# Row norms through GpSimd's power and device memory, and gate rows spread by DMA, in a two-layer fp32 trunk

## The chip, the cores and the metric

One core of a Trainium2 chip runs the whole trunk in one launch. TensorE (PE) multiplies, VectorE (DVE) and ScalarE (ACT) work on tiles, GpSimd (POOL) does masks and fills, and SyncE (SP) issues most transfers. The metric is the device time in microseconds.

## The reference

Input is x of 512 positions by 1024 channels and a memory of 256 positions. Each of two layers adds to x a mixer, an attention over the memory and a gated feed-forward net with a convolution of 3 taps. The mixer of layer 0 is forgetting attention (8 heads) beside differential attention (4 heads); that of layer 1 is an mLSTM of 4 heads. All is float32. What the change touches is how often this is computed, and the rows that go with the heads:

```python
def rms_norm(x, gain):
    x32 = x.astype(jnp.float32)
    y = x32 * lax.rsqrt(jnp.mean(x32 * x32, axis=-1, keepdims=True) + RMS_EPS)
    return (y * gain.astype(jnp.float32)).astype(x.dtype)
...
        logits = logits + F_b[..., :, None] - F[..., None, :]      # forgetting attention
...
        h = num / jnp.maximum(jnp.abs(den), jnp.exp(-m_t))[..., None]   # mLSTM
```

There is a norm ahead of each mixer, memory attention and feed-forward net, one of the memory in each layer, one of each differential head (128 channels), one of each mLSTM head (256 channels), and one at the end. In forgetting attention F is the running sum of a head's log gates; in the mLSTM, m is a running maximum over the positions.

## The kernel before

Activations lie transposed, channels on the 128 partitions and the 512 positions along the free axis, as eight tiles x. A float32 product is made from three matmuls in a reduced format: each operand is split into hi (a cast on ACT) and lo (a subtraction on DVE, L279), and `mm3` (L287 to 291) multiplies hi by hi, hi by lo and lo by hi. So each weight tile comes by a transfer that SP issues (`raw`), becomes `wh` on ACT (L282, L1183, L1352) and `wl` on DVE, each in three buffers, and then goes to PE.

The stages follow one another: mix0 (to about 263 us), xattn0 (to 404), ffn0 (to 740), mix1 (to 963), xattn1 (to 1104), ffn1 (to 1440) and the final norm with the writes. In mix0 four differential heads and four pairs of forgetting heads run beside the preparation of the memory and of both layers' memory keys. In an ffn, 22 blocks of gate and up projections (L1247 to L1420) and their down projections run; most blocks use a Strassen-like scheme of seven products (`c`, `ah`, `al`, `v`, `sa`, `sb` are its tiles).

Two planners write the order. `Plan` (mixers, xattn) takes items with a PE duration, dependences, priorities, buffers and a chain of costs on the other engines; `Sched` (ffn) takes a task for each engine. Both choose by these planned costs what is emitted next; each engine then runs its own queue strictly in order, and an instruction that waits holds all behind it.

A norm of x begins with the squares, summed over the eight tiles into `sq` on DVE (L486). The sum over the partitions and the root go so: four matmuls 128x2 with a matrix of ones put the sums in columns (L417, in the ffn L1218); DVE scales them (L426) and finds the inverse root with three Newton steps (L427 to 432, eleven small instructions more) as a tile of 128x4, position by position. DVE splits that into rh and rl and multiplies each into a diagonal of 128x512 (L446); two matmuls with ones spread it over all partitions (L452); ACT copies it out as `rb` (L456). The projections run on x without the norm, which is multiplied in when their sums leave PSUM (L1057 in xattn, L1317 in the ffn, L1519 in the mLSTM), and there DVE waits for `rb`. The heads' norms go the same way and are read straight from PSUM.

A gate row is spread over the partitions by PE too: `split_rows` (L594 to 604) writes hi and lo into a tile, DVE writes a selector (L611), PE multiplies (L612) and ACT copies the row out (L889 for forgetting heads, L1556 for the mLSTM's `mxb`, L1561 with an exponential for `emt`). On POOL run the causal masks of these rows (L900, L1573). The memory's norm is computed in both layers, from the same squares.

## Time and profile before

| | |
|---|---|
| median of three runs | 1455.0 us (1451.02, 1455.0, 1483.01) |
| profiled execution | 1451.45 us, span 1449.6 us |
| granted TensorE clock | 0.998 |
| PE, PEld, DVE, ACT, POOL busy | 98%, 87%, 82%, 55%, 4% |
| ffn0 and ffn1 | 404 to 740 us and 1104 to 1440 us |

The span is from the first to the last instruction. In rows of a timeline the columns are start, duration, engine, line, operation, output and inputs, shape, and in brackets the idle time of the engine before it with what ended that. In rows of groups, after the bar, stand busy time, mean ns of one, and idle time with its releasers. Matmuls overlap, so a record's duration is longer than the step from one matmul to the next. The trace shows one fp32 matmul as two records.

### The profile page before, as it was taken

The numbers are of one execution on the slowest core, as the hardware profiler recorded it, in microseconds if no ns is written. First come the engines' busy times: TensorE is split into PE (matmuls) and PEld (weight loads), VectorE is DVE, ScalarE is ACT, GpSimd is POOL, SyncE is SP. The second block draws the span as 40 slices with busy tenths as digits, with TensorE's granted clock in tenths as the row PEclk, the third lists the DMA queues.
The fourth block names the chain that finished last, engine by engine and source line by source line (L and its number), as shares of the span: only waits on it lengthen the run. The fifth ranks groups of instructions, "written<-read, shape, count | busy, mean of one in ns | idle before, by whom it ended". The sixth has DMA issues, their size and how long they took to land.

```text
span 1449.6 us, 22210 instructions
## 1 busy us (share of the span) xinstructions
PE 1423.5 (98%) x8330; PEld 1266.7 (87%) x8330; DVE 1189.9 (82%) x2255; ACT 798.5 (55%) x1345; POOL 58.4 (4%) x100
## 2 busy tenths in 40 slices
PE   9999999999999999999999999999999999999998
PEld 7888868899888999989888788889988899998997
DVE  7778886766689999989778868677667999999985
ACT  7767574444466555545456734444445665554544
POOL 0000120000001000000000100000000000000000
PEclk9999999999999999999999999999999999999999
DMA  5222305323247565642332232324323765654322
GB/s 201 88 73 73 102 30 160 117 88 131 83 142 198 152 170 163 164 127 68 90 102 87 74 102 74 116 88 129 119 81 130 187 168 162 172 153 134 92 70 80
DMA packets 60795, 171.74 MB, mean 118 GB/s; under 512 B 6672, under 2 KB 6672, under 8 KB 60688
## 3 DMA queue, kind: packets, MB, share of 16 engines
q1 hardware_dynamic: 55072, 152.43, 32.5%
q0 software_dynamic: 4608, 16.78, 6.9%
q8 instruction: 65, 1.06, 0.3%
q10 hardware_dynamic: 1008, 1.12, 0.2%
q14 instruction: 42, 0.34, 0.1%
HBM read 168.21 MB, written 2.10 MB: 117 GB/s over the span
## 4 chain that ended last, share of the span: by engine, by line
PE 72%; DVE 19%; issue 4%; ACT 3%; DMA 2%; POOL 0%; SPq 0%; DVEq 0%; ACTq 0%; POOLq 0%
PE acc L289 14%; PE acc L291 14%; PE acc L290 14%; DVE wl L279 4%; PE w L289 4%; PE w L291 4%; PE w L290 4%; DVE c L1281 3%; PE acc L351 2%; PE acc L352 2%; PE acc L353 2%; PE s L289 2%; PE s L291 2%; PE s L290 2%; PE w L1620 1%
## 5 line engine op out<-in xcount | busy, mean ns | idle before, releaser
L289 PE MATMUL acc<-xh,wh 128*128 128x512 f32 (+1 forms) x832 | 293.6, 353 | 4.2 <-ACT v L1390 4.2
L291 PE MATMUL acc<-xh,wl 128*128 128x512 f32 (+1 forms) x832 | 289.0, 347 | 0.0
L290 PE MATMUL acc<-xl,wh 128*128 128x512 f32 (+1 forms) x832 | 289.0, 347 | 0.0
L279 DVE TENSOR_TENSOR wl<-raw,wh 128x1024 fp32r<-128x1024 f32 (+2 forms) x201 | 240.3, 1196 | 38.0 <-ACT wh L282 35.8
L282 ACT CAST wh<-raw 128x1024 fp32r<-128x1024 f32 (+2 forms) x137 | 140.3, 1026 | 155.8 <-PE acc L290 96.8
L289 PEld LDWEIGHTS acc<-xh,wh 128*128 128x128 f32 x832 | 158.2, 190 | 19.5 <-ACT v L1390 4.8
L291 PEld LDWEIGHTS acc<-xh,wl 128*128 128x128 f32 x832 | 158.1, 190 | 15.3
L290 PEld LDWEIGHTS acc<-xl,wh 128*128 128x128 f32 x832 | 158.3, 190 | 14.4
L1281 DVE SCALAR_TENSOR_TENSOR c<-hs,vec,c 128x512 f32<-128x512 f32 x176 | 128.8, 745 | 6.6 <-ACT c L1274 6.2
L289 PE MATMUL w<-ah,wh 128*128 128x512 f32 x304 | 115.4, 380 | 0.0
L290 PE MATMUL w<-al,wh 128*128 128x512 f32 x304 | 115.3, 379 | 0.0
L291 PE MATMUL w<-ah,wl 128*128 128x512 f32 x304 | 115.3, 379 | 0.0
L1274 ACT ACTIVATE c<-hs,vec 128x512 f32<-128x512 f32 x88 | 67.9, 808 | 64.2 <-DVE hs L1419 57.1
L291 PEld LDWEIGHTS w<-ah,wl 128*128 128x128 f32 x304 | 57.5, 189 | 8.1
L290 PEld LDWEIGHTS w<-al,wh 128*128 128x128 f32 x304 | 57.6, 190 | 6.7
L289 PEld LDWEIGHTS w<-ah,wh 128*128 128x128 f32 x304 | 57.7, 190 | 6.7
L1295 ACT CAST ah<-c 128x512 fp32r<-128x512 f32 x44 | 27.3, 620 | 65.7 <-DVE c L1291 65.6
L289 PE MATMUL acc<-mem,wh 128*128 128x256 f32 (+1 forms) x192 | 60.3, 314 | 0.0
L291 PE MATMUL acc<-mem,wl 128*128 128x256 f32 (+1 forms) x192 | 59.7, 311 | 0.0
L290 PE MATMUL acc<-mem,wh 128*128 128x256 f32 (+1 forms) x192 | 59.6, 311 | 0.0
L512 DVE TENSOR_TENSOR x<-w,x 128x512 f32<-128x512 f32 x72 | 49.1, 682 | 7.9 <-PE w L291 7.8
L512 DVE TENSOR_TENSOR x<-acc,x 128x512 f32<-128x512 f32 x32 | 22.0, 690 | 40.4 <-PE acc L291 40.4
(373 smaller groups left out, 3766.0 us busy)
## 6 DMA issues: line engine op xcount, KB each, us to landing
raw<-in_up_dram SPq DMA_DIRECT2D x56, 512.0 KB, 3.3
dr<-in_down_dram SPq DMA_DIRECT2D x64, 256.0 KB, 3.4
sa<-in_up_dram SPq DMA_DIRECT2D x32, 512.0 KB, 4.2
sa<-in_up_dram POOLq DMA_DIRECT2D x32, 512.0 KB, 5.5
raw<-in_xk_dram SPq DMA_DIRECT2D x16, 512.0 KB, 3.3
raw<-in_wo_dram SPq DMA_DIRECT2D x16, 512.0 KB, 3.3
raw<-in_xq_dram SPq DMA_DIRECT2D x16, 512.0 KB, 3.3
raw<-in_xv_dram SPq DMA_DIRECT2D x16, 512.0 KB, 3.3
```

The lines of the kernel that those rows point to most:

```text
L279: self.nc.vector.tensor_tensor(out=lo, in0=v, in1=hi.bitcast(F32), op=ALU.subtract)
L282: self.nc.scalar.copy(hi, v)
L289: mm(out, wh, xh, start=first, stop=False, skip_group_check=parts)
L290: mm(out, wh, xl, start=False, stop=False, skip_group_check=parts)
L291: mm(out, wl, xh, start=False, stop=last, skip_group_check=parts)
L351: mm(ps, xh[k][:, ts], wh, start=(k == 0), stop=False)
L352: mm(ps, xh[k][:, ts], wl, start=False, stop=False)
L353: mm(ps, xl[k][:, ts], wh, start=False, stop=(k == 7))
L512: self.nc.vector.tensor_tensor(out=x, in0=restored(ps[:]), in1=x, op=ALU.add)
L1274: nc.scalar.activation(st["c_"][:, j, :], hs()[:, j, 2:514], AF.Identity, scale=self.col("cw", (layer * 3 + 2) * 44 + blk), bias=self.col( ...
L1281: nc.vector.scalar_tensor_tensor(out=c, in0=hs()[:, j, n : n + 512], scalar=w, in1=c, op0=ALU.mult, op1=ALU.add)
L1295: nc.scalar.copy(acts[p][0][:], u())
```

## The change

Eleven of the norms are computed "by rows": those of the four differential heads, of mLSTM heads 0 to 2, and of both layers' xattn and ffn. The summed squares are split into hi and lo (ACT, DVE), two matmuls 128x512 with ones sum them (every partition gets the sums as a row), ACT writes one row of 512 with scale and epsilon, an ACT transfer turns it to 128x4, POOL raises it to the power -0.5, a POOL transfer writes it to device memory, and an SP transfer spreads it over 128 partitions. The remaining norms (first, memory, mix1's, mLSTM head 3, final) stay spread by PE, with POOL's power in place of the Newton steps.

The eight forgetting rows and the mLSTM's two sets of four rows go to device memory by POOL and come back spread by SP, one transfer for a head. The exponential of `emt` is taken once, on four rows. The memory norm is computed in layer 0 only; its roots are kept in device memory and spread again in layer 1. In the ffn the norm is scheduled with a priority ahead of the blocks instead of after the first one. In the plans a chain may hold a pure delay ("-"): 2.7 us for a small transfer and 5.0 for a spread.

```diff
+ROW_DMA, SPREAD_DMA = 2.7, 5.0
...
+    def p_row_norm(self, pl, state, scale, eps, to, fin, deps=(), prio=None, fdeps=(), chain=()):
+
+        nc, sp = self.nc, self.sp
+        st = {}
+
+        def parts():
+            st["p"] = self.row_parts(state["sq"])
+
+        def sums():
+            st["row"] = self.row_sums(st["p"], scale, eps)
+
+        def turned():
+            st["z"] = self.row_turned(st["row"])
+
+        def spread():
+            st["rb"] = self.row_spread(st["d"], to)
+
+        a = pl.add(parts, 0, deps, prio, chain=(("A", 0.52), ("D", 0.6)))
+        a = pl.add(sums, 0.43, [a], prio, take=("s",), free=("s",), chain=(("A", 0.5),))
+        a = pl.add(turned, 0, [a], prio, chain=(("-", ROW_DMA),))
+        a = pl.add(lambda: st.update(d=self.row_root(st["z"])), 0, [a], prio, chain=(("G", 1.05), ("-", ROW_DMA)))
+        a = pl.add(spread, 0, [a], prio, chain=(("-", SPREAD_DMA),))
+        return pl.add(lambda: fin(st["rb"]), 0, [a, *fdeps], prio, chain=chain)
+
+    def row_parts(self, sq):
+        hi, lo = (self.til(self.sp, "sqt", dtype=F32R) for _ in range(2))
+        self.split(hi[:], lo[:], sq[:])
+        return hi, lo
+
+    def row_sums(self, parts, scale, eps):
+        ps = self.bank("b")
+        for i, part in enumerate(parts):
+            self.nc.tensor.matmul(banked(ps[:]), self.onesr[:], alternate(part[:]), start=i == 0, stop=i == 1)
+        row = self.til(self.sp, "sqt")
+        self.nc.scalar.activation(folded(row[0:1, :]), restored(ps[0:1, :]), AF.Copy, scale=float(scale), bias=float(eps))
+        return row
+
+    def row_turned(self, row):
+        z = self.til(self.sp, "z", (P, 4))
+        self.nc.scalar.dma_start(z[:], row[0:1, :].rearrange("o (p j) -> o p j", j=4))
+        return z
+
+    def row_root(self, z):
+        y = self.til(self.sp, "y", (P, 4))
+        self.nc.gpsimd.tensor_tensor(out=y[:], in0=z[:], in1=self.power[:], op=ALU.pow)
+        d = self.til(self.dp, "roots", (1, SEQ))
+        self.nc.gpsimd.dma_start(d[:].rearrange("o (p j) -> (o p) j", j=4), y[:])
+        return d
+
+    def row_spread(self, d, to):
+        rb = self.til(*to)
+        self.nc.sync.dma_start(rb[:], d[0:1, :].to_broadcast([P, SEQ]))
+        return rb
...
     def rsqrt(self, ps, nt, scale, eps):
         nc = self.nc
         z = self.til(self.sp, "z", (P, 4))[:, :nt]
-        zh = self.til(self.sp, "zh", (P, 4))[:, :nt]
         y = self.til(self.sp, "y", (P, 4))[:, :nt]
-        a = self.til(self.sp, "a", (P, 4))[:, :nt]
         nc.vector.tensor_scalar(out=z, in0=ps[:, 0 : 2 * nt : 2], scalar1=float(scale), scalar2=float(eps), op0=ALU.mult, op1=ALU.add)
-        nc.vector.tensor_scalar(out=y.bitcast(I32), in0=z.bitcast(I32), scalar1=-0.5, scalar2=1597463007.0, op0=ALU.mult, op1=ALU.add)
-        nc.vector.tensor_scalar(out=zh, in0=z, scalar1=-0.5, scalar2=None, op0=ALU.mult)
-        for _ in range(3):
-            nc.vector.tensor_tensor(out=a, in0=y, in1=y, op=ALU.mult)
-            nc.vector.tensor_tensor(out=a, in0=a, in1=zh, op=ALU.mult)
-            nc.vector.scalar_tensor_tensor(out=y, in0=a, scalar=1.5, in1=y, op0=ALU.add, op1=ALU.mult)
+        nc.gpsimd.tensor_tensor(out=y, in0=z, in1=self.power[:, :nt], op=ALU.pow)
         return y
...
-    def bcast_cols(self, r, n, pool=None, tag=None, bufs=2):
+    def diag_cols(self, r, n):
...
+    def spread_cols(self, diags, n, pool, tag, bufs=2):
+
+        ps = self.bank("b")
+        for i, dg in enumerate(diags):
+            self.nc.tensor.matmul(banked(ps[:, :n]), self.onesr[:], alternate(dg), start=i == 0, stop=i == 1)
         out = self.til(pool, tag, (P, n), bufs=bufs)
-        nc.scalar.copy(folded(out[:, :n]), restored(ps[:, :n]))
+        self.nc.scalar.copy(folded(out[:, :n]), restored(ps[:, :n]))
...
-    def bcast_row(self, rows, c):
-
-        ps = self.bank("b")
-        s = self.til(self.sp, "sel", (P, P), F32R)
-        self.nc.vector.tensor_copy(s[:], self.selc[:, c : c + 1].to_broadcast([P, P]))
-        self.nc.tensor.matmul(banked(ps[:]), s[:], alternate(rows[:]), start=True, stop=True)
-        return restored(ps[:])
-
+    def spread_row(self, rows, c, tile):
+        self.nc.sync.dma_start(tile[:], rows[c : c + 1, :].to_broadcast([P, SEQ]))
...
+                rows["f"] = self.log_sigmoid_sum(rows["z"], 8, mp, "ta", "tb", "tmp", NTA)
+                rows["d"] = self.til(self.dp, "decays", (8, SEQ), bufs=1)
+                nc.gpsimd.dma_start(rows["d"][:], rows["f"])
...
-                f = self.p_norm(pl, sq, SEQ, (), 1.0 / P, EPS, scaled, [w], p + SOFT_PRIO, chain=(("D", 0.66),))
+                f = self.p_row_norm(pl, sq, 1.0 / P, EPS, (mp, "hrb", (P, SEQ), F32, 1), scaled, [w], p + SOFT_PRIO, chain=(("D", 0.66),))
...
-                        fps = self.bcast_row(rows["f"], h)
-                        fb["b"] = self.til(mp, "ta", bufs=NTA)
-                        nc.scalar.copy(folded(fb["b"][:]), fps)
-
-                    b = pl.add(spread, MM, [g, *qk], p + SOFT_PRIO, take=("s", "ta"), free=("s",), chain=(("A", 0.5),))
+                        fb["b"] = self.til(mp, "fb", bufs=3)
+                        self.spread_row(rows["d"], h, fb["b"])
+
+                    b = pl.add(spread, 0, [g], p, take=("fb",), chain=(("-", SPREAD_DMA),))
...
+        def again():
+            self.memrb = self.til(mp, "memrb", (P, MEM), bufs=1)
+            nc.sync.dma_start(self.memrb[:], self.memd[0:1, :].to_broadcast([P, MEM]))
 
         self.memdone = done
+        if layer:
+            self.memnorm = pl.add(again, 0, done[7], 1, chain=(("-", SPREAD_DMA),))
+            return
...
-            norm = self.x_norm(pl, 0, deps=self.xdone[7])
+            norm = self.x_row_norm(pl, 0, self.xdone[7])
...
+            at = -20.0
+
+            def parts_():
+                n["p"] = [self.til(self.sp, "sqt", dtype=F32R) for _ in range(2)]
+                nc.scalar.copy(n["p"][0][:], prev["sq"][:])
+
+            def low():
+                self.sub(n["p"][1][:], prev["sq"][:], n["p"][0][:])
 
             def sums():
                 n["ps"] = self.bank("s")
-                for i in range(4):
-                    nc.tensor.matmul(n["ps"][:, 2 * i : 2 * i + 2], prev["sq"][:, i * P : (i + 1) * P], self.ones2[:], start=True, stop=True)
+                for i, part in enumerate(n["p"]):
+                    nc.tensor.matmul(banked(n["ps"][:]), self.onesr[:], alternate(part[:]), start=i == 0, stop=i == 1)
+
+            def row():
+                n["row"] = self.til(self.sp, "sqt")
+                nc.scalar.activation(folded(n["row"][0:1, :]), restored(n["ps"][0:1, :]), AF.Copy, scale=1.0 / DM, bias=EPS)
+                n["z"] = self.row_turned(n["row"])
 
             def root():
-                self.r = self.rsqrt(n["ps"], 4, 1.0 / DM, EPS)
+                n["d"] = self.row_root(n["z"])
 
             def spread():
-                self.rb = self.bcast_cols(self.r, SEQ, self.sp, "rb", 1)
-
-            a = pe(0.5, sums, (), [("s", st)])
-            b = add("DVE", 2.1, root, [a], a.prio, (), [("s", st)])
-            s2 = {}
-            c = pe(0.5, spread, [b], [("s", s2)], [("s", s2)])
-            return add("ACT", 0.52, None, [c], c.prio)
+                self.rb = self.row_spread(n["d"], self.rb_to())
+
+            a = add("ACT", 0.52, parts_, (), at)
+            a = add("DVE", 0.6, low, [a], at)
+            a = add("PE", 0.43, sums, [a], at, [("s", st)])
+            a = add("ACT", 0.6, row, [a], at, (), [("s", st)], ROW_DMA)
+            a = add("POOL", 1.05, root, [a], at, (), (), ROW_DMA)
+            return add("SP", 0.1, spread, [a], at, (), (), SPREAD_DMA)
...
+                nc.scalar.activation(mt, mt, AF.Exp, scale=-1.0)
+                gt["rows"] = mx, mt
                 gt["u"] = zi
+                gt["d"] = [self.til(self.dp, n, (H, SEQ), bufs=1) for n in ("mx", "emt")]
+                for d, v in zip(gt["d"], gt["rows"]):
+                    nc.gpsimd.dma_start(d[:], v)
...
-                    mxp = self.bcast_row(gt["rows"], h)
-                    st["mx"] = self.til(mp, "mxb", bufs=1)
-                    nc.scalar.copy(folded(st["mx"][:]), mxp)
-
-                def emts(h=h, st=st):
-                    mtp = self.bcast_row(gt["rows"], 8 + h)
-                    st["emt"] = self.til(mp, "emt", bufs=1)
-                    nc.scalar.activation(folded(st["emt"][:]), mtp, AF.Exp, scale=-1.0)
-
-                b1 = pl.add(most, MM, [uc, qe], p, take=("s",), free=("s",), chain=(("A", 0.5),))
-                b2 = pl.add(emts, MM, [uc, qe], p + 1, take=("s",), free=("s",), chain=(("A", 0.5),))
+                    for i, n in enumerate(("mxb", "emt")):
+                        st[n] = self.til(mp, n, bufs=2)
+                        self.spread_row(gt["d"][i], h, st[n])
+
+                b1 = pl.add(most, 0, [uc, gk, *turn[-1:]], p, chain=(("-", SPREAD_DMA),))
+                turn.append(qe)
...
+                if h < 3:
+                    f = self.p_row_norm(pl, st, 1.0 / 256, 0.0, (mp, "hrb", (P, SEQ), F32, 1), scaled, ns, p + 3, fdeps=oe, chain=(("D", 1.32),))
+                else:
+                    f = self.p_norm(pl, st, SEQ, (mp, "hrb", 1), 1.0 / 256, 0.0, lambda r, rb, st=st: st.update(rb=rb), ns, p + 3)
+                    f = pl.add(lambda scaled=scaled, st=st: scaled(st["rb"]), 0, [f, *oe], p + 3, chain=(("D", 1.32),))
```

PE's order of the ffn's matmuls is the same before and after, but for the norm's. On VectorE, at the start of ffn0, the last of the norm and the first evacuations (hs is a block's sums times rb, c a combination of the Strassen scheme) stood so before:

```order
L441 CAST rh_4293<-y_4274 128x4
L279 TENSOR_TENSOR rl_4294<-y_4274,rh_4293 128x4
L446 TENSOR_TENSOR sqt_4298<-ident,rh_4293 128x512
L446 TENSOR_TENSOR sqt_4301<-ident,rl_4294 128x512
L1317 TENSOR_TENSOR hs_4260<-acc_904_4327,rb_4304 128x512
L1317 TENSOR_TENSOR hs_4260<-acc_912_4367,rb_4304 128x512
L279 TENSOR_TENSOR wl_4420<-raw_4350,wh_4419 128x1024
```

and so now (sq is the squares, split at the second row):

```order
L283 TENSOR_TENSOR sqt_4131<-sq_3887,sqt_4130 128x512
L1329 TENSOR_TENSOR sa_4143<-hs_4127,sa_4143 128x256
L1330 TENSOR_TENSOR sa_4143<-hs_4127,sa_4143 128x256
L283 TENSOR_TENSOR wl_4232<-raw_4188,wh_4231 128x1024
L283 TENSOR_TENSOR tl_4122<-sa_4143,th_4118 128x1024
L283 TENSOR_TENSOR wl_4268<-raw_4199,wh_4267 128x1024
L1388 TENSOR_TENSOR hs_4126<-acc_869_4174,rb_4197 128x512
L1388 TENSOR_TENSOR hs_4126<-acc_878_4216,rb_4197 128x512
L1352 SCALAR_TENSOR_TENSOR c_4248<-hs_4126,vec,c_4248 128x512
L1388 TENSOR_TENSOR hs_4127<-acc_884_4254,rb_4197 128x512
```

The Newton steps and diagonals are gone, and the splits of two weights stand ahead of the first evacuation, as before; that of wl_4313, which had stood behind two evacuations, comes behind three. On ScalarE, at the same place, the new rows stand among the weight casts:

```order
L1420 CAST a22h_4193<-ra_4155 128x512
L1275 CAST sqt_4130<-sq_3887 128x512
L1241 CAST wh_4231<-raw_4188 128x1024
L1287 ACTIVATE sqt_4145<-s_4138 1x512
L1331 CAST th_4118<-sa_4143 128x1024
L426 DMA z_4147<-sqt_4145 128x1x4
L1241 CAST wh_4267<-raw_4199 128x1024
L1345 ACTIVATE c_4248<-hs_4126,vec 128x512 x2
```

The 1x512 row of the norm comes behind the cast of wh_4231, and its transfer behind the cast of th. In xattn0, VectorE had this order ahead of the first query (tmp is a query's sums times rb):

```order
L441 CAST rh_2988<-y_2943 128x4
L279 TENSOR_TENSOR rl_2989<-y_2943,rh_2988 128x4
L446 TENSOR_TENSOR sqt_2993<-ident,rh_2988 128x512
L446 TENSOR_TENSOR sqt_2996<-ident,rl_2989 128x512
L1057 SCALAR_TENSOR_TENSOR tmp_3007<-acc_614_2923,rb_2999 128x512
L279 TENSOR_TENSOR ql_632_3010<-tmp_3007,qh_631_3009 128x512
L1057 SCALAR_TENSOR_TENSOR tmp_3019<-acc_623_2975,rb_2999 128x512
L1033 TENSOR_TENSOR tmp_3025<-acc_533_2456,memrb_1833 128x256
L279 TENSOR_TENSOR wl_3073<-raw_3071,wh_3072 128x1024
```

and has this now:

```order
L283 TENSOR_TENSOR wl_2909<-raw_2907,wh_2908 128x1024
L283 TENSOR_TENSOR ktl_2788<-tmp_2877,kth_2787 128x256
L283 TENSOR_TENSOR wl_2927<-raw_2925,wh_2926 128x1024
L1115 SCALAR_TENSOR_TENSOR tmp_2943<-acc_586_2806,rb_2905 128x512
L1115 SCALAR_TENSOR_TENSOR tmp_2949<-acc_592_2841,rb_2905 128x512
L283 TENSOR_TENSOR wl_2957<-raw_2955,wh_2956 128x1024
L283 TENSOR_TENSOR ql_614_2946<-tmp_2943,qh_613_2945 128x512
```

The first evacuation is followed by the second, and the low part of a value weight (wl_2957) stands behind both. In mix1, ScalarE had the first convolution (cv, th, q) ahead of the mask's exponential (mk):

```order
L282 CAST wh_8344<-raw_8343 128x1024
L1522 ACTIVATE cv_8233<-hs_8230,vec 128x512
L1526 ACT_TABLE_LOAD
L1526 ACTIVATE th_8238<-cv_8233 128x512
L282 CAST wh_8406<-raw_8405 128x1024
L1529 ACTIVATE q_8241<-cv_8233 128x512
L1522 ACTIVATE cv_8277<-hs_8274,vec 128x512
L1556 COPY mxb_8304<-s_8300 128x512
L1561 ACTIVATE emt_8310<-s_8306 128x512
L1576 ACTIVATE mk_8362<-mk_8362,ucol_8189 128x512
L1576 ACTIVATE mk_8371<-mk_8371,ucol_8189 128x384
```

and now it has the exponential first:

```order
L286 CAST wh_8123<-raw_8122 128x1024
L286 CAST wh_8167<-raw_8166 128x1024
L1644 ACTIVATE mk_8179<-mk_8179,ucol_8020 128x512
L1595 ACTIVATE cv_8064<-hs_8061,vec 128x512
L1644 ACTIVATE mk_8188<-mk_8188,ucol_8020 128x384
L1599 ACTIVATE th_8069<-cv_8064 128x512
L1595 ACTIVATE cv_8108<-hs_8105,vec 128x512
L286 CAST wh_8233<-raw_8232 128x1024
```

The copy of mxb is gone, and the exponential for the first mask has moved ahead of the first convolution step of head 0.

110 lines of the change are left out of this document (53 added, 57 removed).

## The prediction

> **What bounds the kernel now.** I read the page's first three parts, then the busy time by stage, then the idle time ahead of the lines that the diff touches, and at last the order in time at the places where the new norms sit.
>
> ```profile
> span 1449.6 us, 22210 instructions
> PE 1423.5 (98%) x8330; PEld 1266.7 (87%) x8330; DVE 1189.9 (82%) x2255; ACT 798.5 (55%) x1345; POOL 58.4 (4%) x100
> PE 72%; DVE 19%; issue 4%; ACT 3%; DMA 2%; POOL 0%; SPq 0%; DVEq 0%; ACTq 0%; POOLq 0%
> ```
>
> TensorE is busy 98% of the span and carries 72% of the chain that ended last; VectorE has 19% of that chain. So an instruction taken from PE counts in full, one taken from VectorE hardly, and a longer wait counts where PE runs dry behind it. The busy time by stage (columns: stretch, length, then PE, PEld, DVE and ACT busy) says where that is near:
>
> ```profile
> 0.00:263.00 263.00, 255.61 (x1311) 212.66 (x1312) 209.69 (x578) 172.96 (x349) 18.62 (x39) 0.99 0.32 104
> 263.00:404.00 141.00, 140.96 (x763) 125.54 (x762) 94.31 (x175) 66.60 (x121) 0.14 (x2) 1.00 0.32 105
> 404.00:740.00 336.00, 330.53 (x2175) 306.11 (x2175) 312.94 (x496) 185.25 (x282) 14.38 (x18) 1.00 0.51 139
> 740.00:963.00 223.00, 220.88 (x1064) 185.75 (x1063) 166.45 (x317) 116.84 (x180) 11.37 (x23) 1.00 0.29 94
> 1104.00:1440.00 336.00, 331.60 (x2240) 308.66 (x2239) 308.76 (x501) 186.62 (x288) 13.71 (x16) 1.00 0.49 133
> ```
>
> PE is nearly full everywhere. In the two ffn stages DVE has 312.94 and 308.76 of 336 us: there it has little room to catch up. In xattn (94.31 of 141) it has much.
>
> **What leaves PE.** First the small sums of squares (four 128x2 matmuls; the trace has two records for each), and the pitch of a 128x512 matmul, at the start of the first ffn:
>
> ```profile
> 408.18 1.05 PE L1218 MATMUL s<-ones,sq 128*128 128x2 f32 x8
> 409.09 0.46 PE L290 MATMUL acc<-xl,wh 128*128 128x512 f32 x1
> 416.27 0.38 PE L452 MATMUL s<-sqt,ones 128*128 128x512 f32 x1
> 416.48 0.38 PE L290 MATMUL acc<-xl,wh 128*128 128x512 f32 x1
> 416.68 0.58 ACT L456 COPY rb<-s 128x512 f32<-128x512 f32 x1 [4.42 <-PE s L452]
> 417.30 1.29 DVE L1317 TENSOR_TENSOR hs<-acc,rb 128x512 f32<-128x512 f32 x2 [1.24 <-ACT rb L456]
> L612 PE MATMUL s<-rows,sel 128*128 128x512 f32 x16 | 6.1, 410 | 0.1
> ```
>
> One norm's sums hold PE 0.91 us (408.18 to 409.09); a row of 128x512 moves on every 0.21 us (416.27 to 416.48), though its record lasts 0.38. Eleven norms of four and the second memory norm with two go: 11.5 x 0.91 = 10.5 us. The 16 gate-row matmuls (L612) go: 16 x 0.21 = 3.4 us, and two 128x256 of the second memory norm, 0.2. A row norm's two 128x512 sums stand for the two diagonal matmuls that it loses: 0. Together **-14.1 us**.
>
> With them go waits of PE for the diagonals:
>
> ```profile
> L452 PE MATMUL s<-sqt,ones 128*128 128x512 f32 x28 | 11.3, 428 | 2.9 <-DVE sqt L446 2.6
>   DVE sqt L446: 9.3, 18
> ```
>
> The group row gives 2.9 us of idle PE, the row of the line's own waits 9.3 with its weight loads (18 times). The true figure is between; I take 5 for 16 norms, and 12 of the 16 no longer wait there: **-4** (ends -2 and -7).
>
> The root becomes one POOL instruction. No row shows it. The nearest are the small POOL fill and the mask instructions, all far larger than 128x4, and the DVE rows that it replaces:
>
> ```profile
> L1518 POOL MEMSET hs<- 128x3 f32 x8 | 0.8, 99 | 123.6 <-DVE cv L1524 102.0 <-DVE a L430 21.6
> L900 POOL TENSOR_SCALAR_AFFINE_SELECT tb<-ta x32: 292/512/1432, 142.8 to 218.3; 128x128 f32<-128x128 f32 x8, 128x256 f32<-128x256 f32 x8, 128x384 f32<-128x384 f32 x8, 128x512 f32<-128x512 f32 x8
> 1441.49 0.16 DVE L426 TENSOR_SCALAR z<-s 128x2 f32<-128x2 f32 x1 [0.76 <-PE s L417]
> 1443.45 0.16 DVE L432 SCALAR_TENSOR_TENSOR y<-a,y 128x2 f32<-128x2 f32 x1
> ```
>
> Between 0.1 and 1.4 us; a power is no plain pass, so I take 1.0, near the upper end. The Newton steps took 1441.49 to 1443.61, 2.1 us, so the norms that stay spread by PE are about 1 us quicker. On the path that is so in the first norm, where nothing else is ready, and in the last, half hidden behind transposes: **-1.5** (0 to -3). The DVE work saved beside it (these steps, the diagonals, 16 selector casts) is hidden by PE: 0. So are the dropped copies on ACT (55% busy).
>
> **What the row norm's chain costs.** Squares to hi (cast) and lo, sums, row, transfer to 128x4, power, transfer to device memory, spread. The transfers do not exist yet; the nearest:
>
> ```profile
> out_dram<-th ACTq DMA_DIRECT2D x4, 256.0 KB, 2.4
> vec<-in_vec_dram ACTq DMA_DIRECT2D x1, 4.0 KB, 3.1
> ra<-in_up_dram SPq DMA_DIRECT2D x32, 256.0 KB, 3.5
> sa<-in_up_dram POOLq DMA_DIRECT2D x32, 512.0 KB, 5.5
> L1336 POOL DMA_DIRECT2D sa<-in_up_dram x32 | 27.5, 860 | 516.3 <-DMA sa<-in_up_dram 186.4 <-DVE c L1291 71.1 <-DVE sb L1358 65.9
> L1295 ACT CAST ah<-c 128x512 fp32r<-128x512 f32 x44 | 27.3, 620 | 65.7 <-DVE c L1291 65.6
> L279 DVE TENSOR_TENSOR wl<-dr,wh 128x512 fp32r<-128x512 f32 x64 | 43.7, 683 | 0.0
> ```
>
> Small transfers land after 2.4 to 3.1 us; I take 2.8 for the turn to 128x4 and 2.8 after 0.86 us of issue on POOL for the roots (POOL's own queue shows 5.5, for 512 KB: the upper end). The spread writes 256 KB: 3.5. So 0.62 + 0.68 + 0.43 + 0.58 + 2.8 + 1.0 + 0.86 + 2.8 + 3.5 = 13.3 us (11 to 17). The old chain in xattn 0 went from the end of the squares to the first use of rb (rows below), 267.24 to 274.56: 7.3. Each row norm's result is **6 us later** (4 to 10).
>
> The Trainium skill ("DMA: Bandwidth & Descriptors", Anatomy of one DMA) gives a transfer a fixed 2.0 us, most of it the receipt of the last write. By that figure each of the two small transfers would be 0.8 us shorter than I take; an estimate from it is a chain 1.6 us shorter and a sum some 12 us lower. The rows above, 2.4 and 3.1 for 256 and 4 KB, decide.
>
> **Where the 6 us go.** In each ffn VectorE holds the evacuation of the first block's sums until rb is there, as it did before; nothing in its queue may pass. The new rows stand in order on ACT too: the 1x512 row and its transfer come behind a weight cast whose buffer the earlier block frees. So rb, and the evacuation of 417.30, comes at about 422.6 to 425. DVE has its earlier splits done by 418.5 and then idles about 4 us more than the 1.24 us that the row above shows. It is nearly full until the first Strassen block, where PE already waits for it:
>
> ```profile
> 450.39 0.69 DVE L1358 TENSOR_TENSOR sb<-sa,raw 128x512 f32<-128x512 f32 x1 [1.24 <-DMA sa<-in_up_dram]
> 452.86 0.38 PE L289 MATMUL acc<-xh,wh 128*128 128x256 f32 x1 [2.69 <-ACT v L1390]
> ```
>
> DVE has 1.24 us of slack there, behind a transfer, so not all is passed on. I take 4 us in each ffn, **+8** (+2 to +14).
>
> In xattn the loss is another. Between the evacuations of the first queries and a value weight's low part the order puts no other work:
>
> ```profile
> 266.56 0.68 DVE L486 TENSOR_TENSOR sq<-sq,sqt 128x512 f32<-128x512 f32 x1
> 274.56 0.69 DVE L1057 SCALAR_TENSOR_TENSOR tmp<-acc,rb 128x512 f32<-128x512 f32 x1 [1.19 <-ACT rb L456]
> 277.53 1.22 DVE L279 TENSOR_TENSOR wl<-raw,wh 128x1024 fp32r<-128x1024 f32 x1
> ```
>
> With rb at 280.5, two evacuations of 0.69 and the low part of 1.22 end at about 283. In the changed order PE has 56 matmuls, 12.1 us, between the row sums (about 269.7, with the hops between the engines) and that weight's first use: it gets there at 281.8. It waits some 1.5 to 3 us; I take 2.3, in two layers **+4.6** (0 to +10).
>
> In mix1 the running maximum of the input gate goes to device memory and comes back spread:
>
> ```profile
> 767.65 0.68 DVE L1491 TENSOR_TENSOR num<-th,mk 4x512 f32<-4x512 f32 x1
> 774.39 0.72 ACT L1522 ACTIVATE cv<-hs,vec 128x512 f32<-128x512 f32 x1 [0.95 <-DVE hs L1519]
> 786.10 1.13 PE L1579 MATMUL s<-q,k 128*128 128x512 f32 x2 [0.44 <-ACT k L1529]
> ```
>
> It is ready at 767.65; issue 0.86, landing 2.8, spread 3.5 and a mask of 1.4 give 776.2. In ACT's new order the exponential of that mask stands ahead of head 0's first convolution step, which ran at 774.39: that chain is 2.5 us later, and the keys' with it. The first score already waited 0.44 us for the keys. Some of the 2.5 is caught up between the two convolutions: +1.5. Three heads' norms then stop DVE's queue for some 3 us each, with 166.45 of 223 us busy; a third reaches PE: +3. **+4.5** (0 to +10). In mix0 four diff heads' norms do the same, at 209.69 of 263; POOL's queue holds masks behind the powers, and the gate rows' eight spreads join SP's queue, early. **+2** (-2 to +6).
>
> SP's queue gets 29 more transfers of up to 256 KB, about 3.5 us each, at a DMA share of at most 0.51. I cost them at nothing: weights are fetched several tiles ahead of PE; if that cover went, a late tile would cost up to 3.5 us. The memory norm's second spread needs its roots from layer 0, long there: 0. The ffn's norm being scheduled first moves no matmul of the blocks.
>
> **The sum.** -14.1 - 4 - 1.5 + 8 + 4.6 + 4.5 + 2 = -0.5. The profiled execution took 1451.45 us (its span and 1.85 around it), so **1451**; the median shown, 1455.0, lies 3.5 above it and the fastest, 1451.02, at it. Within 2% (29 us either way of 1455, about what a measurement of this kernel can tell from no change) is 1426 to 1484.
>
> **Rivals.** 1. The waits are hidden: DVE makes up its loss before the first Strassen block, and xattn's weight is not needed so early. Then 14 of the 19 us of new waits go: 1437. For it: DVE's slack outside ffn, 1.24 us behind a transfer; against: PE's 2.69 us wait there.
>
> 2. Faster by over 2%: waits hidden wholly, and less DVE work also ends other PE waits (7.4 us idle in mix0, 5.5 and 4.4 in the ffns, rows of the stages). 1451.45 - 19.6 - 8 = 1424. Against: in the ffns the change takes only some 3 us from DVE.
>
> 3. Longer hops: each chain is 2 us longer than taken, as POOL's 5.5 us landing would have it. A us of chain costs about 7.5 us in all (2 ffns, 2 xattns, about 3.5 among mix1's and mix0's norms): 1466.
>
> 4. The other side: a slow power. If it holds POOL 4.4 us longer than taken, 4.4 x 7.5 = 33 us bring 1484; from 5.4 us an instruction on it decides. At 6 it is 5 x 7.5 = 37.5: 1489. Against: the longest POOL instruction of the masks row is 1.43 us, for 128 times the elements; for it: none of those rows is a power. The Trainium skill ("GPSIMD Engine Reference", 2.1 Instruction dispatch) says that the first call of a freshly loaded routine costs about 6 us with no instruction to show it; paid once per run it would be lost in the range, paid at each norm, where powers and masks alternate, it would be this rival. No row here shows such a load.
>
> **Chances.** The waits about as worked out (1443 to 1460) 0.45; rival 1 0.17; rival 2 0.08; rival 3 0.18; rival 4 0.12. Leaving out rivals 2 and 4, the range is 1430 to 1480; the forecast's own range is 1443 to 1460. Faster than 1426: 0.08. Slower than 1484: 0.12. Within: 0.80.
>
> **What would show it.** PE's instructions: no line for the 128x2 sums in the ffns, 16 selector matmuls gone, PE busy lower by about 14 us. DVE's first evacuation in ffn 0 some 5 to 8 us after 417.30 counted from the squares, and PE's wait at the first Strassen block about 6 to 7 us instead of 2.69; if it stays below 4, rival 1 holds. In xattn a PE wait on a low weight about 12 us after the row sums. The power's own duration settles rival 4, the landing of the roots rival 3. The forecast is wrong if the spread lands late because SP's queue holds it behind weight transfers that wait for buffers, which I cost at nothing.

## The result, and the profile after

The changed kernel takes 1454.1 us (median of 22 executions, 1448.94 to 1460.15), the kernel before 1450.8 us (22, 1447.71 to 1483.01). The ratio is 1.0027, 95% interval 1.0015 to 1.0038: slower by 0.3%, inside the range and inside 2%, but on the other side of zero than the forecast (1451 against the 1455.0 then shown; by the sum, -0.5 us). The execution of 1483.01 us was a slow one, and the ratio leaves it out.

The profile page of the changed kernel, its first two lines, and its transfers that are new (bytes, then us from issue to landing):

```profile
span 1450.7 us, 21782 instructions
PE 1411.1 (97%) x8220; PEld 1258.2 (87%) x8220; DVE 1144.7 (79%) x1980; ACT 795.3 (55%) x1334; POOL 86.8 (6%) x129
...
z<-sqt ACTq DMA_DIRECT2D x11, 2.0 KB, 2.0
roots<-y POOLq DMA_DIRECT2D x11, 2.0 KB, 1.8
rb<-roots SPq DMA_DIRECT2D x4, 256.0 KB, 4.7
hrb<-roots SPq DMA_DIRECT2D x7, 256.0 KB, 4.1
```

PE is busy 12.4 us less (1423.5 before), and the span is 1.1 us longer: 13.5 us more in which PE stands. The three hops of a row norm were priced at 2.8, 2.8 and 3.5 and took 2.0, 1.8 and 4.1 to 4.7 in the median. The power's own line:

```profile
L431 POOL TENSOR_TENSOR y<-z,power x11: 1009/1034/1757, 111.8 to 1112.0; 128x4 f32<-128x4 f32 x11
```

Its median, 1.03 us, is the 1.0 that the prediction took. The longer ones, 1.2 to 1.8 us, are five of the seven in the mixers. Rivals 3 and 4 fall with these two readings.

By stage (from the last addition to x of a stage to that of the next, in ffn1 to the last one of the full form x<-w, profiled executions; the prediction's terms sorted by stage below them):

| us | mix0 | xattn0 | ffn0 | mix1 | xattn1 | ffn1 to its last addition | end | span |
|---|---|---|---|---|---|---|---|---|
| before | 263.5 | 141.2 | 335.2 | 222.6 | 141.2 | 303.2 | 42.7 | 1449.6 |
| changed | 256.7 | 141.7 | 338.3 | 223.9 | 142.4 | 305.5 | 42.3 | 1450.7 |
| difference | -6.8 | +0.5 | +3.1 | +1.3 | +1.2 | +2.3 | -0.4 | +1.1 |
| prediction | -5.6 | +1.0 | +2.8 | -1.9 | +1.0 | +2.8 | -0.5 | -0.5 |

In these two executions the stages went nearly as worked out, but for mix1. In the first ffn, VectorE holds its first evacuation for the spread row, which stands at the end of these lines (in brackets, idle time before it):

```profile
401.21 0.68 DVE L552 TENSOR_TENSOR sq<-sq,sqt 128x512 f32<-128x512 f32 x1
403.01 0.68 DVE L283 TENSOR_TENSOR sqt<-sq,sqt 128x512 fp32r<-128x512 f32 x1
410.53 1.23 DVE L283 TENSOR_TENSOR wl<-raw,wh 128x1024 fp32r<-128x1024 f32 x1 [2.93 <-ACT wh L1241]
415.71 1.29 DVE L1388 TENSOR_TENSOR hs<-acc,rb 128x512 f32<-128x512 f32 x2 [3.95 <-DMA rb<-roots]
```

From the end of the squares (401.89) to the evacuation it is 13.8 us; before it was 9.2 (408.12 to 417.30). At the first Strassen block PE then waits three times, 3.2 us together, where it was 2.69:

```profile
442.59 0.38 PE L293 MATMUL s<-th,wh 128*128 128x256 f32 x1 [0.54 <-ACT wh L1420]
444.66 0.38 PE L295 MATMUL s<-th,wl 128*128 128x256 f32 x1 [1.57 <-DVE wl L283]
446.19 0.58 PE L293 MATMUL acc<-xh,wh 128*128 128x256 f32 x1 [1.05 <-ACT v L1458]
```

In xattn0 VectorE idles for rb, and PE then for the value weight behind it:

```profile
274.71 1.29 DVE L1115 SCALAR_TENSOR_TENSOR tmp<-acc,rb 128x512 f32<-128x512 f32 x2 [5.10 <-DMA rb<-roots]
277.19 0.48 PE L356 MATMUL acc<-wl,mem 128*128 128x512 f32 x1 [1.72 <-DVE wl L283]
```

In mix1 the third head's spread row holds VectorE with the last head's convolution behind it, until PE stands 3 us for that head's keys:

```profile
879.11 0.75 DVE L1701 SCALAR_TENSOR_TENSOR num<-num,vec,hrb 128x512 f32<-128x512 f32 x1 [3.02 <-DMA hrb<-roots]
885.01 0.63 ACT L1602 ACTIVATE k<-cv 128x512 f32<-128x512 f32 x1 [1.10 <-DVE cv L1600]
885.69 2.08 PE L1647 MATMUL s<-q,k 128*128 128x512 f32 x2 [3.00 <-ACT k L1602]
```

What no step of the prediction held is seen in stretches of the trace (columns as in the prediction: PE, PEld, DVE, ACT and POOL busy, then the granted clock). These are the changed kernel behind the first Strassen block's waits, and behind the one just shown:

```profile
436.00:441.00 5.00, 5.00 (x27) 4.42 (x26) 5.00 (x9) 2.59 (x4) 0.39 (x1) 1.00 0.92 255
441.00:446.00 5.00, 2.03 (x14) 1.45 (x12) 5.00 (x8) 3.87 (x6) 1.33 (x2) 0.93 0.81 184
446.00:448.00 2.00, 1.81 (x8) 1.81 (x9) 1.61 (x3) 1.10 (x3) 0.00 (x0) 0.50 0.96 262
448.00:450.00 2.00, 2.00 (x12) 2.00 (x11) 1.28 (x3) 1.40 (x3) 0.00 (x0) 0.50 1.06 222
450.00:455.00 5.00, 4.85 (x33) 4.66 (x33) 4.76 (x8) 2.14 (x4) 0.86 (x1) 0.78 0.47 152
...
882.00:884.00 2.00, 0.69 (x4) 0.26 (x2) 2.00 (x3) 1.23 (x2) 0.00 (x0) 1.00 0.00 0
884.00:886.00 2.00, 0.31 (x1) 0.31 (x2) 1.97 (x4) 0.63 (x1) 0.00 (x0) 0.92 0.23 80
886.00:888.00 2.00, 2.00 (x3) 0.86 (x3) 0.92 (x3) 0.62 (x1) 0.00 (x0) 0.50 0.47 182
888.00:890.00 2.00, 2.00 (x7) 1.39 (x6) 1.05 (x2) 0.51 (x1) 0.69 (x2) 0.73 0.00 0
```

After the wait the granted clock is 0.50, and only three matmul records start in the 2 us from 886. PE counts as busy there, at half its pace. The clock's missing share, doubled, is the time at half clock: 0.08 of 2 us, 0.50 of 2 and 0.27 of 2 make 3.4 us behind the last head's wait, and the shares from 441 to 455 make 6.9 us at the Strassen block. The kernel before, at its wait of 2.69 us in the same block, kept its clock:

```profile
449.00:453.00 4.00, 1.31 (x12) 1.12 (x11) 2.76 (x6) 2.44 (x5) 0.84 (x1) 1.00 0.51 158
453.00:455.00 2.00, 2.00 (x19) 2.00 (x20) 1.99 (x4) 1.65 (x3) 0.86 (x1) 1.00 0.89 125
```

Over all executions the mean clock is 0.9932 for the changed kernel (22, from 0.990 to 0.997) and 0.998 for the kernel before (the 83 executions beside the experiments). The fastest execution of the changed kernel, 1448.94 us, had 0.997; the two slowest, 1460.15 and 1459.77, 0.991 and 0.992. A line through the 22 gives 1.35 us for 0.001 of clock; if PE's work filled the whole time, 0.001 of 1454 would be 1.45.

**Theory C**, then: the work removed and the waits added were about right; the waits cost a second time by the clock that they lower, some 0.005 of 1450 us, or 7 us. **Rival D**: the waits are the whole cost, and the clock only shows them. **Rival B**: the loss comes by other means, the added transfers and the new order of the instructions. **Theory A**, the prediction's own, puts the ffn's loss on the row that comes late.

### The profile page after: what moved, and what is told of

Its sections match the earlier page's. It is cut to its first block, busy times and chain, and to the rows that moved or that the text cites. A ratio compares the mean times of both kernels' runs of the same rounds, so it can differ in the third digit from the quotient of the medians.

```text
span 1450.7 us, 21782 instructions
## 1 busy us (share of the span) xinstructions
PE 1411.1 (97%) x8220; PEld 1258.2 (87%) x8220; DVE 1144.7 (79%) x1980; ACT 795.3 (55%) x1334; POOL 86.8 (6%) x129
## 3 DMA queue, kind: packets, MB, share of 16 engines
q8 instruction: 64, 1.05, 0.3%
```

## The experiments

Each is compared with the kernel before on the same chip; the clock is the mean of its executions. The kernel before took 1449.6 to 1450.8 us on these chips, so a difference between two experiments, or to the changed kernel, can be off by about 1 us.

| kernel | median us | ratio, 95% interval | clock |
|---|---|---|---|
| changed | 1454.1 | 1.0027, 1.0015 to 1.0038 | 0.993 |
| 1 ffn norms by PE, power | 1453.5 | 1.0021, 1.0008 to 1.0034 | 0.994 |
| 2 xattn norms by PE | 1450.2 | 0.9994, 0.9981 to 1.0008 | 0.996 |
| 3 mLSTM heads by PE | 1454.3 | 1.0026, 1.0016 to 1.0037 | 0.994 |
| 4 three more powers | 1493.6 | 1.0297, 1.0277 to 1.0316 | 0.979 |
| 5 all of 1 to 3 | 1446.4 | 0.9979, 0.9970 to 0.9988 | 0.996 |
| 6 before, power alone | 1449.9 | 0.9997, 0.9988 to 1.0005 | 0.998 |
| 7 three waits filled | 1454.5 | 1.0033, 1.0021 to 1.0046 | 0.996 |
| 8 as 5, Newton in the ffn | 1440.1 | 0.9932, 0.9918 to 0.9945 | 0.998 |
| 9 waits filled, other place | 1461.4 | 1.0078, 1.0062 to 1.0094 | 0.993 |
| 10 ffn alone as before | 1450.1 | 0.9999, 0.9988 to 1.0010 | 0.996 |
| 11 one wait filled | 1453.4 | 1.0019, 1.0008 to 1.0029 | 0.994 |

### 1 to 3: one kind of norm taken back

In 1 the ffn's norm is again the text of before, with the power as its root. The edits of 1, 2 and 3, of the first its order:

```diff
-            a = add("ACT", 0.52, parts_, (), at)
...
+            a = pe(0.5, sums, (), [("s", st)])
+            b = add("DVE", 2.1, root, [a], a.prio, (), [("s", st)])
+            s2 = {}
+            c = pe(0.5, spread, [b], [("s", s2)], [("s", s2)])
...
-            norm = self.x_row_norm(pl, 0, self.xdone[7])
+            norm = self.x_norm(pl, 0, deps=self.xdone[7])
...
-                if h < 3:
+                if h < 0:
```

> The changed kernel with the two ffn norms spread by TensorE again, as before (small sums, diagonals, two matmuls), with GpSimd's power as the root. Theory A (a row norm's longer chain holds VectorE's queue, and the first Strassen block passes the loss on): the ffn stages go back from 338.3 and 305.5 us to about 335.2 and 303.2, TensorE's wait at the first Strassen block falls from about 3.7 to at most 2.9 us, and the whole comes to about 5.4 us below the changed kernel, 0.999 of the kernel before. Rival B (the loss is spread by other means: a lower clock, more transfers in the queues): the ffn stages keep most of their loss, total within 2 us of the changed kernel.

> The changed kernel with both xattn norms spread by TensorE again. Theory A: the wait of 1.9 and 2.5 us on a value weight's low part goes, 0.9 us of small sums comes back in each layer; stages 141.7 and 142.4 go to about 141.1, the whole 1 to 2 us below the changed kernel. Rival B: no change of those stages beyond 0.3 us.

> The changed kernel with the norms of the first three mLSTM heads spread by TensorE again, as that of the fourth. Theory A (each such norm holds VectorE's queue about 3 us for the spread row, and the keys' convolution of the next head stands behind it): the 3.2 us wait of TensorE for the last head's keys goes to below 1, 2.7 us of small sums come back, mix1 goes from 223.8 to about 222 to 223 us. Rival B (mix1 lost its time at the start, by the spread of the gate rows): the wait at the last head's first score stays, and mix1 grows by the 2.7 us.

The first came out against theory A in the whole, 0.6 us in place of 5.4. Of its signs in the profile, PE's wait at the Strassen block did fall below 2.9 us (2.46 and 2.13, from 3.2 and 3.1), but of the ffn stages only the first came part of the way back: 336.3 and 305.6 us. The second gave 4 us, more than the 1 to 2 expected: its stages went to 140.7 and 140.7 and the clock rose by 0.002. The 141.7 and 142.4 of the changed kernel are low: over the seven kernels with the row norm in xattn and its chain not lengthened (changed, 1, 3, 7, 9, 10, 11) the fourteen stages take 141.7 to 145.8, 143.4 in the mean, and in seven of them part of the time is at half clock. In the third mix1 did fall, to 221.4 us, and the wait for the last head's keys was under 0.7, as theory A has it; but the whole stayed, with longer stages of xattn (144.4 in the second layer, behind a PE wait of 2.86) and of mix0. Single executions differ from one another by some us a stage, according to which waits brought the half clock with them, so the medians tell what one kind is worth, and the profiles only where.

### 4: a longer chain

```diff
-        self.nc.gpsimd.tensor_tensor(out=y[:], in0=z[:], in1=self.power[:], op=ALU.pow)
+        for _ in range(4):
+            self.nc.gpsimd.tensor_tensor(out=y[:], in0=z[:], in1=self.power[:], op=ALU.pow)
```

> The changed kernel with the power of the eleven row norms taken four times instead of once (same result each time), which makes each chain 3.1 us longer and nothing else. By the prediction's rate, 7.5 us for a us of chain, it is 23 us slower than the changed kernel: about 6 in the two ffns, 6 in the two xattns, 6 in mix1, 5 in mix0. The rival (the chains lie mostly beside slack): under 8 us.

It is 39.5 us slower than the changed kernel. In the two profiled executions, 40.7 us apart, PE is idle for 67.6 us in place of 39.6, 28.0 more, where the rate of 7.5 us gave 23; and while it is busy it loses 17.8 us to half clock in place of 6.1, 11.7 more (busy time times the clock's missing share, summed over stretches of 2 us). At the last head's first score, in rows of stretches:

```profile
904.00:908.00 4.00, 4.00 (x20) 3.30 (x18) 0.22 (x1) 1.04 (x1) 0.00 (x0) 1.00 0.66 169
908.00:912.00 4.00, 0.15 (x1) 0.00 (x0) 3.96 (x7) 0.66 (x2) 0.00 (x0) 0.81 0.07 28
912.00:914.00 2.00, 0.00 (x0) 0.00 (x0) 1.98 (x3) 0.90 (x2) 0.00 (x0) 0.50 0.00 0
914.00:916.00 2.00, 1.64 (x2) 0.84 (x3) 1.30 (x2) 0.92 (x2) 0.00 (x0) 0.50 0.71 262
916.00:918.00 2.00, 2.00 (x6) 1.22 (x5) 1.16 (x3) 0.33 (x1) 0.40 (x1) 0.68 0.00 0
```

The clock falls within the wait (0.81 in its first 4 us) and returns some 3 us after work does; the time at half clock is 6.8 us, twice 3.4. The Trainium skill ("TensorE: Matmul & The Clock Gate", Part 1) states this: the array falls to half rate after an idle window of about 3.4 us. The half rate agrees with the 0.50 of these rows; the length does not bound it, as the changed kernel lost its clock after a wait of 3.00 us, and experiment 10 (below) after one of 1.92.

### 5 and 6: all three kinds back, and the power alone

Experiment 5 is the edits of 1, 2 and 3 together; 6 is the kernel before with this:

```diff
-        for _ in range(3):
...
+        nc.gpsimd.tensor_tensor(out=y, in0=z, in1=self.power[:, :nt], op=ALU.pow)
```

> The changed kernel with the ffn, xattn and mLSTM norms all spread by TensorE again; by rows remain only the four differential heads; gate rows by DMA, one memory norm and GpSimd's power stay. Theory C (beside each wait of TensorE the changed kernel pays for a granted clock of 0.5 for 3.4 to 6.8 us after a wait of about 3 us or more, which no step of the prediction holds): with the waits of ffn, xattn and mix1 below 3 us the mean clock comes back from 0.993 to about 0.997 and the time to about 1446 us, 0.997 of the kernel before. Rival D (the waits alone, no clock): the norms' 7.3 us of small sums come back, waits of about 15 us go: 1447 with the clock still at 0.993 to 0.994. Rival B (spread transfers and order): 1453 or more.

> The kernel before with the three Newton steps replaced by one GpSimd power, nothing else. By the prediction's step: each root about 1 us earlier, of which 1.5 us in all lies on the path at the first and last norms, and part of the waits for the diagonals goes: 2 to 4 us faster, 0.997 to 0.999. If VectorE's relief counted beside that, 5 us or more.

Experiment 5 met theory C in time and nearly in clock: 1446.4 us at 0.996, 8 us below the changed kernel and faster than the kernel before. Rival D's 1447 is as near, and a clock that rises as the waits go fits a clock that only shows them too; so this run does not part C from D. The power alone is worth nothing (0.9997), against 2 to 4 us expected. Its profile says why: mix0 is 2.1 us shorter, mix1 0.9 and each xattn 0.5, but the ffn stages are longer, 336.1 and 305.4.

### 7, 9 and 11: the waits filled

The same chains, but with matmuls that nobody reads in the place of PE's waits, into a bank that the next group overwrites. In 11, only ahead of the last head's first score; in 7 and 9 also at the first Strassen block of each ffn, 11 ahead of its third group or, as the second piece shows, 18 ahead of its second:

```diff
                         ps = self.bank("s")
+                        if h == 3 and s == 0:
+                            for _ in range(13):
+                                nc.tensor.matmul(banked(ps[:]), self.onesr[:], alternate(self.xh[0][:]), start=True, stop=True)
...
+                    junk = self.bank("b")
+                    for _ in range(18):
+                        nc.tensor.matmul(banked(junk[:]), self.onesr[:], alternate(self.xh[0][:]), start=True, stop=True)
```

> The changed kernel with 13 matmuls that nobody reads ahead of the last mLSTM head's first score and 11 ahead of the first Strassen block's third group in each ffn, into banks that the next group overwrites: TensorE is busy where it waited before. Theory C: the real work starts no earlier, but the clock stays at 1.0 behind these places, the mean clock rises from 0.993 to about 0.996 or more, and the kernel is 3 to 5 us faster than the changed one. Rival D (no cost beside the waits): no faster, or slower by what the matmuls overrun the waits, up to 1 us at each place.

> The changed kernel with 18 matmuls that nobody reads (3.9 us) directly ahead of the first Strassen block's second group in each ffn, where TensorE waits for v, and 13 ahead of the last mLSTM head's first score. Theory C (half clock after a wait of about 3 us): the clock is 1.0 behind these places, v comes no later, the mean clock rises to about 0.996, and the kernel is 3 to 5 us faster than the changed one, about 1450 us. Rival D: equal time, or up to 1 us more at each place.

> The changed kernel with only the 13 unread matmuls ahead of the last mLSTM head's first score. Theory C: the clock behind that place is 1.0 instead of 0.5 for about 3.4 us, mix1 goes from 223.9 to about 222 us and the kernel is 1.5 to 2.5 us faster than the changed one, at 1452 us. Rival D: mix1 stays at 223.9 or grows by up to 0.5 us.

In the ffn the filling failed as an instrument. TensorE's groups came out in another order around the added matmuls, and the wait for VectorE and ScalarE came back a little later: in ffn0 3.3 us in experiment 7, 1.95 and 3.2 in experiment 9, whose ffn stages grew to 343.5 and 310.1. So 7 and 9 say nothing on the clock in the ffn. At the last head it did work, alone in 11 as in 7 and 9. First the filled place, then the clock over it, in experiment 11:

```profile
882.25 2.97 PE L1648 MATMUL s<-xh,ones 128*128 128x512 f32 x13
885.35 1.77 PE L1650 MATMUL s<-q,k 128*128 128x512 f32 x4
```

```profile
882.00:884.00 2.00, 2.00 (x11) 1.73 (x11) 2.00 (x4) 1.23 (x2) 0.00 (x0) 1.00 0.00 0
884.00:886.00 2.00, 1.87 (x8) 1.15 (x7) 1.66 (x4) 0.91 (x2) 0.00 (x0) 1.00 0.43 133
886.00:888.00 2.00, 2.00 (x9) 1.39 (x8) 1.62 (x3) 0.34 (x1) 0.26 (x1) 1.00 0.32 129
```

The clock is 1.00 where it was 0.50, and nine records start in the 2 us from 886 in place of three. The first score begins 3.1 us behind the start of the filling, as long as the wait was; it comes no sooner. Mix1 is 222.9 us here and 221.7 in experiments 7 and 9, against 223.9. The whole is 0.7 us faster in the median and 1.4 in the mean (1453.2 against 1454.7), with 0.0009 more clock, 1.3 us: theory C's direction, below the 1.5 to 2.5 expected, and the two intervals overlap.

Two traces part C from D at this place without any added matmul. Mix1's code is the same in experiment 1 as in the changed kernel, and PE's wait for the last head's keys was longer there (3.24 us), but the clock held. The changed kernel first, then experiment 1:

```profile
880.00:890.00 10.00, 7.00 (x22) 4.58 (x21) 7.91 (x12) 2.99 (x5) 0.69 (x2) 0.83 0.14 52
880.00:890.00 10.00, 7.07 (x31) 5.70 (x32) 8.16 (x14) 4.66 (x8) 0.69 (x2) 1.00 0.19 59
```

PE is busy as long in both, with 22 matmul records in the one and 31 in the other. From the last head's first score to the end of mix1 it takes 74.9 us in the changed kernel and in experiment 2, both with 3.4 us at half clock, and 73.1 to 73.2 in experiments 1, 3, 7, 9, 10 and 11, where the clock held. So the half clock costs 1.7 us beside the wait, and rival D is out at this place.

### 8 and 10: the order in the ffn

Experiment 8 is 5 with the Newton steps for the ffn's two roots; 10 takes back nothing but the ffn's norms, Newton steps and all:

```diff
-                self.r = self.rsqrt(n["ps"], 4, 1.0 / DM, EPS)
+                self.r = self.rsqrt(n["ps"], 4, 1.0 / DM, EPS, True)
```

> The kernel of three kinds by TensorE, with the Newton steps on VectorE for the two ffn norms as well, so that the ffn stages hold the instructions of the kernel before. If the power is what keeps the ffn stages of that kernel at 336.6 and 306.3 us (the kernel with the power alone has 336.1 and 305.4, the kernel before 335.2 and 303.2), they go back by 1 to 3 us each and the whole comes to about 1443 us, 0.995 of the kernel before. If the 303.2 of the kernel before was one good execution, the time stays within 1 us of 1446.4.

> The changed kernel with only the two ffn norms as before: spread by TensorE, and with the Newton steps on VectorE. If the order of VectorE, ScalarE and TensorE in front of the first Strassen block is what the ffn stages lost by (it was another with the row norm and with the power), the stages are 334 to 335 and 303 us again, and the kernel comes 5 to 7 us below the changed one, about 1448 us, where the same undoing with the power as the root gave 1453.5. If the row norm's late result was the cause and the power costs nothing there, it is again 1453 to 1454.

Experiment 8 is the fastest kernel of the study: 1440.1 us, 0.9932 of the kernel before. The two Newton roots make 6 us against experiment 5, a little more than the 1 to 3 a stage expected; the ffn stages are 334.3 and 302.9, 2.3 and 3.4 us shorter. Experiment 10 gave 4.0 us against the changed kernel, less than the 5 to 7 expected, where undoing the same norms with the power (1) had given 0.6. In its profiled execution, one of its slowest (1452.43 us), ffn1 came back to 303.8 but ffn0 took 337.7 us, not 334 to 335: PE waited 1.92 us at the Strassen block, and half clock followed for 3.4 us (the clock is the third number from the end):

```profile
440.00:450.00 10.00, 8.08 (x50) 7.43 (x49) 9.22 (x15) 6.02 (x10) 1.71 (x2) 0.93 0.79 197
450.00:460.00 10.00, 9.85 (x80) 9.66 (x78) 9.00 (x15) 4.70 (x9) 0.13 (x1) 0.90 0.82 239
```

By the medians, then, most of the ffn's loss is not the late row: in experiment 1 the row came early, and the time hardly fell. From the end of the squares, in the profiled executions:

| us after the squares | first evacuation, ffn0 and ffn1 | v of the first Strassen block, ffn0 and ffn1 |
|---|---|---|
| before | 9.2, 9.2 | 44.3, 42.7 |
| changed (row norm) | 13.8, 13.8 | 43.9, 43.8 |
| 5 (PE, power) | 7.2, 7.2 | 44.3, 44.6 |
| 8 (PE, Newton) | 9.2, 9.2 | 42.7, 42.7 |
| 10 (PE, Newton) | 9.2, 9.2 | 43.5, 42.7 |

v is the ScalarE copy for which PE waits at the Strassen block. In experiment 5 rb is there 2 us sooner than in 8, and v is 1.6 to 1.9 us later. VectorE's queue in experiment 5 shows another order:

```profile
406.49 0.68 DVE L1376 TENSOR_TENSOR hs<-acc,rb 128x512 f32<-128x512 f32 x1
408.06 1.54 DVE L1340 SCALAR_TENSOR_TENSOR c<-hs,vec,c 128x512 f32<-128x512 f32 x2 [0.88 <-ACT c L1333]
409.51 0.68 DVE L1376 TENSOR_TENSOR hs<-acc,rb 128x512 f32<-128x512 f32 x1
410.11 1.22 DVE L283 TENSOR_TENSOR wl<-raw,wh 128x1024 fp32r<-128x1024 f32 x1
412.38 1.54 DVE L1340 SCALAR_TENSOR_TENSOR c<-hs,vec,c 128x512 f32<-128x512 f32 x2 [1.05 <-ACT c L1333]
```

The early evacuations stand singly, each followed by work that waits about 1 us for ScalarE; in 8, as before, the first two stand together. Whether this makes v late is not shown. Just ahead of the block VectorE also stands 1.22 us for a transfer of weights (sa, at 437.35), and 0.9 to 1.6 us in both ffns of experiments 1, 5 and 6, but not in 8. PE's wait at the block differs too:

```profile
444.01 0.48 PE L293 MATMUL acc<-xh,wh 128*128 128x256 f32 x1 [2.35 <-ACT v L1449]
```

```profile
443.46 0.38 PE L293 MATMUL acc<-xh,wh 128*128 128x256 f32 x1 [1.05 <-ACT v L1459]
```

The first row is of experiment 5, the second of 8: PE waits 2.35 us for v in the one and 1.05 in the other. This holds over all traces whose ffn waits are not filled and whose chains are not lengthened. With the order of before (before, 8, 10) PE waits 1.05 us there in four of six ffn stages, 2.69 and 1.92 in the two where a transfer comes late, and one of the six has half clock; with another order (changed, 1, 2, 3, 5, 6, 11) it waits 2.1 to 3.5 us in the fourteen stages, and eleven have it.

## Why the prediction was right, and where it failed

**What bounds the kernel, and what leaves PE.** Right, and short in size: PE busy fell by 12.4 us by its records where 14.1 had been worked out, but records at half clock are longer than the work in them. At full clock the work fell by 16.9 us (table below), 8.9 of it in mix0.

**The chain of a row norm.** Right in its sum: 13.3 worked out, 13.8 measured in the ffn. The parts differed: the small transfers were 0.8 to 1.0 us shorter each than taken, the spread 0.6 to 1.2 longer. The fixed 2.0 us of the Trainium skill ("DMA: Bandwidth & Descriptors", Anatomy of one DMA), which the prediction set aside for the rows, was the better price of the small ones (2.0 by ScalarE's queue and 1.8 by GpSimd's, the path for which that section gives it). The 12 us that the prediction drew from it did not come, as the longer spread and the steps ahead of the power (5.6 us for 5.1) gave them back.

**xattn and mix0.** Right in the profiled execution: +0.5 and +1.2 for +1.0 each, -6.8 for -5.6. In xattn that is luck of the execution: the waits are as long as worked out (1.72 and 2.37 us for 2.3), but half clock follows them in about half of the stages, and the mean of fourteen is 2.2 us above the kernel before. Mix0 holds most of the change's gain, and experiments 5 and 8 keep it (255.1 and 256.2 us); no run took its parts singly, other than the power, 2.1 us in experiment 6.

**ffn.** Right in number, wrong in cause, so the number is luck. The +4 us of wait was put on the late row. The row was later by 4.6 us in place of 6, and v by 1.1 us in ffn1; in ffn0 v was not later at all, as the execution before had its own late transfer there. So the 2.69 us that the prediction took as the wait of before was the long one; in ffn1 it was 1.05. The wait at the Strassen block, 3.2 us, is below the 4 that the prediction had set as the mark of rival 1: the late row was mostly made up, as that rival has it, and the stage was longer all the same: in ffn0 PE was idle only 0.2 us longer than before and lost 3.1 us to half clock; in ffn1 the clock held, and PE was idle 2.4 us longer. Experiment 1 takes the lateness away and most of the loss stays, and 10 takes the order back and 4 us go in the median. What the step left out is that with rb ready at another time, early or late, the order on VectorE up to the first Strassen block is another, and with each other order traced PE waited longer there than the 1.05 us that the order of before gives when no transfer is late.

**mix1.** Too small: "a third reaches PE: +3". The stage is 3.2 us longer than its terms. The wait for the last head's keys is 3.00 us by itself, and the clock behind it takes 1.7 us again. In the whole stage PE is idle 5.0 us longer than before, where the terms gave 3.2 (4.5 of waits less 1.3 saved).

**The sum.** This is the step that failed: it adds waits as if PE went on afterwards at the pace of before, with no term for the half clock behind them. The profiled executions come apart as follows, summed over stretches of 2 us; lost at half clock is PE's busy time times the clock's missing share, and work is the rest:

| us | work | PE idle | lost at half clock | span |
|---|---|---|---|---|
| before | 1421.9 | 26.1 | 1.6 | 1449.6 |
| changed | 1405.0 | 39.6 | 6.1 | 1450.7 |
| 4 | 1405.9 | 67.6 | 17.8 | 1491.4 |
| 5 | 1409.3 | 29.3 | 4.8 | 1443.4 |
| 8 | 1409.5 | 27.6 | 1.7 | 1438.8 |

The idle time grew by 13.5 us, which is what the sum holds (19.1 of new waits less the 5.5 saved, 13.6). The work fell by 16.9 for 14.1. Work and idle time alone would make the change 3.4 us faster; the 4.5 us more at half clock, which no term held, make it 1.1 slower. The profiled execution of the changed kernel is one with a high clock (0.995); over all 22 the lost share against the kernel before is 0.005 of 1450, or 7 us, an estimate that takes all of it for PE's work. That the waits came out right in total is partly luck, since single stages were off both ways: 2.5 us too low in mix0, 1.8 in mix1, and 3.5 too high in ffn0.

**Open.** Which waits cost the clock is not settled. Half clock followed waits of 1.92 us (ffn0 of experiment 10), 1.96 us (xattn0 of experiment 11) and 3.00 us (the last head), and did not follow 2.69 us (ffn0 of the kernel before) or 3.24 us (the last head of experiment 1). Nor is it shown why the order in the ffn comes out better with the slower root, nor whether the order itself or the transfer that VectorE waits for makes PE's wait longer.

## What to carry to other kernels

When work is taken from a full TensorE at the price of waits, price each wait of some 2 us or more twice: its own length, and some 1.7 us (half of 3.4) for the half clock that may follow. Take a change with many places apart by place: here the same change was worth -7 us in mix0 and cost time in the ffns and xattns, and keeping the row norms in mix0 alone, with the gate rows by DMA, one memory norm and the power outside the ffns, made 0.993 of the kernel before (experiment 8). Where a scheduler sets each queue's order by when things are ready, compare the order at the next bound place: here a root that was ready 2 us earlier went with another order and a slower kernel.

## What the runs showed of the hardware

After a wait of 3.00 us the granted TensorE clock was 0.50 for 3.4 us, and after one of 3.24 us at the same place, in experiment 1, it was 1.00; the half clock made the stretch behind it 1.7 us longer. At a wait of 6.20 us it was 0.50 for 6.8 us, the end of the wait included. GpSimd's power on 128x4 took 1.01 to 1.04 us, up to 1.8 us in the mixers and 1.94 us the first time; no row shows anything near the 6 us that the Trainium skill ("GPSIMD Engine Reference", 2.1 Instruction dispatch) gives for the first call of a freshly loaded routine. Nor is there room for it in a gap: that first power began at 17.97 us, 0.25 us after the start of the VectorE instruction that it waits for. A transfer of 2 KB landed after 2.0 us in the median (1.9 to 3.4) from partition 0 to 128 partitions and after 1.8 (1.7 to 4.5) from 128 partitions to device memory, and a spread of a norm's row of 2 KB over 128 partitions after 3.4 to 5.1 us.
